# A fifth raw-weight place, down rows queued behind the last product, and three wide tiles in the first feed-forward

## The chip, the cores and the metric

The kernel runs on one core of one Trainium2 chip. The core has a matrix engine (TensorE, PE in the profile, its weight loads PEld), a vector engine (VectorE, DVE), a scalar engine (ScalarE, ACT), GpSimd (POOL) and SyncE (SP); each takes its instructions from a queue in order. SP issues nearly all of the loads. The metric is the device time of one execution in microseconds, as the median of several runs.

## What is computed

A decoder layer on 512 tokens of width 1024, in float32: a feed-forward, a mixer (dilated attention and a gated linear recurrence side by side), and a second feed-forward, each between two RMS norms and added to the residual with the factors of the reference.

```python
def swiglu(x, w_gate, w_up, w_down):
    return (jax.nn.silu(x @ w_gate) * (x @ w_up)) @ w_down

f = swiglu(rms_norm(h, ffn1_norm_pre[l]), ffn1_w_gate[l], ffn1_w_up[l], ffn1_w_down[l])
h = h + 0.5 * rms_norm(f, ffn1_norm_post[l])
u = rms_norm(h, mix_norm_pre[l])
proj = u @ w_in[l]
...
h = h + rms_norm(merged @ w_out[l], mix_norm_post[l])
f = swiglu(rms_norm(h, ffn2_norm_pre[l]), ffn2_w_gate[l], ffn2_w_up[l], ffn2_w_down[l])
h = h + 0.5 * rms_norm(f, ffn2_norm_post[l])
```

D_FF is 2816, so the gate and up matrices have 22 tiles of 128 columns each.

## The kernel before

**Numbers.** Every operand of a large product is split into a high part and a low part (`split`, lines 302 to 304: a copy on ACT at 303, a subtraction on DVE at 304), and a product is high x high + high x low + low x high, three matmuls of the same place.

**Seven products.** A gate tile and an up tile, over two halves of the 1024 inputs and two halves of the 512 tokens, form a 2 x 2 block product that is done with seven products p1 to p7 in place of eight. The operands of the seven are sums and differences of the quarters: of the activations once (`x_forms`, `forms_of`), of the weights for each tile (`w_forms`, line 685: four adds on DVE and four splits). A tile's weight forms take three places of `w8` (of four) and one of `w4`.

A tile's seven products come in two forms with the same result. The narrow one (`seven_on`, line 734) has for each product and each of four k three matmuls of 256 columns (lines 730 to 732), 84 in all, and works in four half-banks of PSUM; ACT copies a half-bank at line 744 four times, DVE adds at 970 and 975. The wide one (`seven_wide`, line 765) has for each k one matmul of 512 columns, the high weights on the high and the low activations side by side (782), and one of 256 (783), 56 in all, and works in five whole banks. There a product's value is the sum of a bank's halves: ACT moves a bank to another at 788 (`move`, three times a tile), copies a half at 794 and DVE adds the other half at 796 (`fold`, four times), and `sum_of` makes two adds at 804 and 806 (twice). Both run p1, p5, p6, p2, p7, p3, p4; the third product writes on the bank of a copy that was taken behind the first, the fifth and the seventh likewise behind the third and the fifth.

**Feed-forward.** `ffn_order` (67) writes out the order: the first 6 tiles of the first feed-forward (3 of the second) as plain products, then for every tile f the weight forms of tile f + 1 (`prep`), the tile's seven products (`prod`, 961), and behind them a step of the down projection. The 22 rows of down are in parts 0 to 3 (16 rows, also done as seven products, `down7`, 1055: rows of three matmuls of 512 columns at 1065 to 1067) and a last part of 6 rows, which `last_product` does behind all tiles. The steps of a part are done behind the tiles in `STEPS_AT`; in the first feed-forward part 1 stands behind tiles 9 to 12, part 2 behind 13 to 16, part 3 behind 17 to 20. A step needs the weight forms of `d_forms` (991) and its start values, which ACT puts into the `aux` banks at 1053; its results go to the `ea` tile or to `facc` at 1070.

**What sets the order.** The framework's scheduler queues the instructions of each engine ahead of time, by a precedence that follows the program's text and by when its own model takes them to be ready. `tc.high_priority(offset=n)` moves a block forward by n; weight forms have 100 (`AHEAD`), copies out of PSUM 200 (`EVAC`). `tc.issue_after(x)` puts the block's instructions on the engine of x behind x in its queue, without a wait. In the second feed-forward three such edges exist: the rows of `down7` stand behind `state["product"]`, the last product so far (1064); the weight forms of the next tile stand behind the last split of `d_forms` (1110 to 1111, 1104 to 1107); and the late activation forms behind the last copy (`rest`, 939 to 944). None of the three is in the first.

**Loads.** The weights come as one stream of blocks of 128 x 1024 in the order of use (`stream_plan`, `raw_of`, 235). Each goes on SP to one of four places `raw`; the load waits until DVE and ACT have read what stood there. The first 8 blocks, of 512 columns, are loaded by `fetch_start` (278) into the four places, but for the very first, which has a tile `first_t` together with the small constants `sm`. The first norm's sum of squares `acc` and its root `r1` have a pool of their own, `npool`. `r1` is read last by the plain tile 5 (956 and 958).

Of the kernel before, what the change touches and what calls it, by code (L numbers as in the profile page):

```python
# [10 lines left out]
F32 = mybir.dt.float32  # L11
# [5 lines left out]
P = 128  # L17
T = 512
# [2 lines left out]
NF = 22  # L21
FF_PARTS = ((0, 4), (4, 8), (8, 12), (12, 16), (16, 22))
NSTD = {1: 6, 2: 3}
WIDE = {1: (), 2: (9, 13, 17)}

SEVEN = range(4)
STEPS_AT = {1: ((6, 7, 7, 8), range(9, 13), range(13, 17), range(17, 21)),
# [3 lines left out]
EPS = 1e-6  # L31
HB = 256
RAW_W = 1024
NEG = -1.0e30

FIRST_ON = {1: 5, 2: 5}
# [67 lines left out]
def stream_plan():  # L104

    plan = []

    def down(n, a, half):
        for kk in range(part_blocks(a)):
            plan.append((("down", n, a, half, kk), 1024))  # L110

    def ffn(n):
        for ev in ffn_order(n):
            if ev[0] == "std":
                plan.append((("gate", n, ev[1]), 1024))
                plan.append((("up", n, ev[1]), 1024))
            elif ev[0] == "prep":
                plan.append((("gu", n, ev[1]), 2048))
            elif ev[0] == "prepd":
                for q in SEVEN_RAW[ev[2]]:  # L120
                    plan.append((("dq", n, ev[1], q), 1024))
        for half in range(2):
            down(n, len(FF_PARTS) - 1, half)

    def qk(h):
        for g in range(NG):
            plan.append((("pair", g * 4 + h, 12 + g * 4 + h), 2048))

    ffn(1)
    del plan[:4]  # L130
    for k in range(KC):
        plan.insert(k, (("start", k), 512))
    for k in range(4):
        plan.append((("v", 0, k), 1024))
    for q in ("g0", "g1", "u0", "u1"):
        plan.append((("vq", q), 2048))
    for h in range(NH):
        qk(h)
    for c in range(0, KC, 2):
        plan.append((("pair", 52 + c, 53 + c), 2048))  # L140
    for m in range(0, KC, 2):
        plan.append((("attn", m), 1024))
    for what, h in LRU_ORDER:
        if what == "gates":
            plan.append((("lru", h), 1024))
        elif (what, h) in PAIRED:
            plan.append((pair_key(what, h), 2048))
        else:
            for c in GATE1[h] if what == "gate1" else (2 * h, 2 * h + 1):
                plan.append((("in", COLUMN[what] + c), 1024))  # L150
    for m in range(KC):
        plan.append((("rec", m), 1024))
    for half in range(2):
        for kk in range(4):
            plan.append((("out", half, kk), 1024))
    ffn(2)

    return [(key + (i,), RAW_W) if width > RAW_W else (key, width)
            for key, width in plan for i in (("lo", "hi") if width > RAW_W else ("",))]


def stream_groups():

    groups, cur, w = [], [], 0
    for key, width in stream_plan():
        if w + width > RAW_W or (cur and cur[0][0][0] == "start"):
            groups.append(cur)
# [12 lines left out]
SMALL_W = _o  # L180
# [4 lines left out]
def hybrid_layer(ctx: ExitStack, tc: tile.TileContext, xT: bass.AP, xN: bass.AP, wst: bass.AP,  # L185
# [4 lines left out]
    cpool = ctx.enter_context(tc.tile_pool(name="cpool", bufs=1))  # L190
    bpool = ctx.enter_context(tc.tile_pool(name="bpool", bufs=6))
    wpool = ctx.enter_context(tc.tile_pool(name="wpool", bufs=4))
    tpool = ctx.enter_context(tc.tile_pool(name="tpool", bufs=4))
    npool = ctx.enter_context(tc.tile_pool(name="npool", bufs=1))
    psum = ctx.enter_context(tc.tile_pool(name="psum", bufs=1, space=bass.MemoryType.PSUM))
    dpool = ctx.enter_context(tc.tile_pool(name="dpool", bufs=1, space=bass.MemoryType.DRAM))

    first_t = cpool.tile([P, 512 + SMALL_W], F32, name="first")
    sm = first_t[:, 512:]
    cst = cpool.tile([P, CONST_W], F32, name="cst")  # L200
    ones = cpool.tile([P, P], F32, name="ones")
    eps = cpool.tile([P, 1], F32, name="eps")
# [6 lines left out]
    def hm(m, sl=slice(0, T)):  # L209

        return hs["t"][m // 4][:, m % 4, sl]
# [21 lines left out]
    state = {"g": 0, "i": 0, "off": 0, "raw": None, "ahead": AHEAD, "split": None}  # L233

    def raw_of(key, dst=None):

        g, i = state["g"], state["i"]
        grp = groups[g]
        if i == 0:
            w = grp[-1][1] + grp[-1][2]  # L240
            raw = dst if dst is not None else wpool.tile([P, RAW_W], F32, name="raw", tag="raw", bufs=4)
            src = bass.AP(tensor=wst.tensor, offset=wst.offset + state["off"], ap=[[w, P], [1, w]])
            nc.sync.dma_start(raw[:, :w], src)
            state["raw"] = raw
            state["off"] += w * P
        k, o, w = grp[i]
        assert k == key, (k, key)
        src = state["raw"][:, o:o + w]
        if i + 1 == len(grp):
            state["g"], state["i"] = g + 1, 0  # L250
        else:
            state["i"] = i + 1
        return src

    def raw_two(key, dst=None):

        return [raw_of(key + (n,), None if dst is None else dst[:, i * RAW_W:(i + 1) * RAW_W])
                for i, n in enumerate(("lo", "hi"))]
# [10 lines left out]
    def w8():  # L269
        return wpool.tile([P, 2, 1024], F32R, name="w8", tag="w8", bufs=4)  # L270
# [6 lines left out]

    def fetch_start():

        raws = [wpool.tile([P, RAW_W], F32, name="raw", tag="raw", bufs=4) for _ in range(4)]  # L280
        wts = []
        for k in range(KC):
            raw = raws[k // 2][:, (k % 2) * 512:(k % 2) * 512 + 512]
            if k == 0:
                raw = first_t[:, :512]
                nc.sync.dma_start(hm(k), xT[k])
                nc.sync.dma_start(raw, first[:, :512])
            else:
                nc.sync.dma_start(raw, bass.AP(tensor=wst.tensor, offset=wst.offset + (k - 1) * 512 * P,
                                               ap=[[512, P], [1, 512]]))  # L290
                nc.sync.dma_start(hm(k), xT[k])
            if k % 2 == 0:
                wt = w8()
            o = (k % 2) * 512
            wts.append((wt[:, 0, o:o + 512], wt[:, 1, o:o + 512], raw))
        state["g"], state["off"] = KC, (KC - 1) * 512 * P
        return wts
# [14 lines left out]
    def tmp(name):  # L312
        return tpool.tile([P, T], F32, name=name, tag="t")
# [255 lines left out]
    def act_of(his, los):  # L569
        return Act([his[k // 4][:, k % 4, :] for k in range(8)], [los[k // 4][:, k % 4, :] for k in range(8)])  # L570
# [293 lines left out]
    def ffn(n, x, r, forms_x, apool, pss):  # L864
# [96 lines left out]
        def prod(f, w):  # L961
            g, u = tmp("g"), tmp("u")
            if f in WIDE[n]:
                seven_wide(t, w, *([x[:, h] for h in HALVES] for x in (g, u)), then=forms_left)
# [69 lines left out]
        def sum_at(p):  # L1034
            if p in outs:
                o, half, sign = outs[p]
                return quarter(o, half), sign
            return acts["ea"][:, extra.index(p)], 1.0

        def follows(a, p):  # L1040

            return a > 0

        def groups(i):
            return [(p, k) for p in SEVEN_STEPS[i] for k in range(2)]
# [9 lines left out]
        def down7(a, i, w):  # L1055
            x = sevens[a]
            gs = groups(i)
            for m, (p, k) in enumerate(gs):
                ps = seeded.pop((p, k))
                first = not follows(a, p)  # L1060
                for j in range(2):
                    xh, xl = (x[p][:, s_, j * HB + k * P:j * HB + k * P + P] for s_ in range(2))
                    wh, wl = (w[p][:, s_, j * T:(j + 1) * T] for s_ in range(2))
                    with tc.issue_after(state["product"]) if n == 2 else nullcontext():
                        PE.matmul(ps, xh, wh, start=first and j == 0, stop=False, skip_group_check=True)  # L1065
                        PE.matmul(ps, xh, wl, start=False, stop=False, skip_group_check=True)  # L1066
                        PE.matmul(ps, xl, wh, start=False, stop=j == 1, skip_group_check=True)  # L1067
                dst, sign = sum_at(p)
                with tc.high_priority(offset=EVAC):
                    ACT.activation(dst[:, k], ps, AF.Copy, scale=sign)  # L1070
                    if m + 3 < len(gs):
                        seed(a, *gs[m + 3])
            if a == SEVEN[-1]:
                merge(i)
# [64 lines left out]
    ap1 = ff1.enter_context(tc.tile_pool(name="act1", bufs=1))  # L1139
    new_h()  # L1140
    u1 = act_of(*act_two(ap1))
    acc = npool.tile([P, T], F32, name="acc", tag="acc", bufs=1)
    nc.scalar.dma_start(sm, first[:, 512:])
    warm(eps)

# [2 lines left out]
        PE.matmul(wu[:, :P], ones, ones, start=True, stop=True)  # L1148
    wts = fetch_start()
    pss = [acc_ps() for _ in range(4)]  # L1150
    r1 = npool.tile([P, T], F32, name="r", tag="r", bufs=1)
    for k in range(KC):
        wh, wl, raw = wts[k]
        if k == 0:
# [598 lines left out]
    grow5, _ = gains(ap2, 4)  # L1753
# [26 lines left out]
def _bias(table):  # L1780
# [10 lines left out]
    for hd in range(NH):  # L1791
        for g, (sl, s, d, m) in enumerate(((slice(0, 256), s0, 1, m0), (slice(256, 384), s1, 4, m1),
                                           (slice(384, 512), s1, 4, m2))):
            vals = table[:, g * 4 + hd][_bucket(np.maximum(s, 0) * d)]
            res[hd, :, sl] = np.where(m, vals, np.float32(NEG))
    return res
# [95 lines left out]
```

## Time and profile before

| | us |
|---|---|
| median of 3 runs | 1206.48 (1205.55 to 1207.29) |
| the profiled execution | 1206.06 |
| its span, first to last instruction | 1204.3 |
| PE busy in the span | 1196.5 |
| DVE busy | 1039.5 |
| ACT busy | 838.7 |
| POOL busy | 26.1 |

The span is what the rows of the trace cover; 1.76 us of the execution lie around it. A row of a group reads: line, engine, operation, out<-in by the program's names, shapes, count, then the busy time and the mean duration in ns, and the idle time of the engine ahead of it with what ended it. A row of the timeline has start and duration first. A row of a stretch has its bounds, its length and the busy time of PE, PEld, DVE, ACT and POOL (instructions in brackets), then the granted clock, the DMA share and GB/s. Matmuls are pipelined: the time that one costs is the distance between two starts, not its duration.

### The profile page before, as it was taken

To read this page: it belongs to the slowest core of one execution; us is meant where nothing else is said; L and a number is where in the kernel's file an instruction comes from. 1 tells how busy PE (TensorE), PEld (TensorE's weight loads), DVE (VectorE), ACT (ScalarE), POOL (GpSimd) and SP (SyncE) were. 2 spreads that over 40 slices of the span, in tenths; PEclk is the share of its full clock that TensorE was granted. 3 is DMA by queue.
4 is the path that set the end of the run, shared out by engine and by line. 5 is a ranking of instruction groups with operands and counts; after the bars stand their busy time and mean duration, and the time that the engine had idled before them with its cause. 6 is when DMAs were issued, how large, how long until landed. Compare 5 with 4: busy or idle time off the path is not lost.

```text
span 1204.3 us, 18736 instructions
## 1 busy us (share of the span) xinstructions
PE 1196.5 (99%) x7138; PEld 1065.4 (88%) x7138; DVE 1039.5 (86%) x1641; ACT 838.7 (70%) x1455; POOL 26.1 (2%) x51
## 2 busy tenths in 40 slices
PE   9999999999999999999999999999999999999997
PEld 8899999999888889888888888888899989898996
DVE  7999888889689899999978899874798888889974
ACT  7566787887566676777836988734566687878763
POOL 0000000000011000000000000000100000000000
PEclk9999999999999999999999999999999999999999
DMA  7234343434725232322323432235443333333441
GB/s 268 88 95 132 126 140 108 139 111 153 248 102 165 71 97 88 97 82 86 107 73 119 170 115 100 80 113 189 144 141 106 123 123 123 123 125 122 140 176 70
DMA packets 45819, 149.77 MB, mean 124 GB/s; under 512 B 5152, under 2 KB 8608, under 8 KB 45728
## 3 DMA queue, kind: packets, MB, share of 16 engines
q1 hardware_dynamic: 38160, 131.09, 33.5%
q0 software_dynamic: 7280, 17.30, 4.3%
q8 instruction: 56, 0.92, 0.3%
q14 instruction: 35, 0.29, 0.1%
q10 hardware_dynamic: 288, 0.17, 0.0%
HBM read 138.06 MB, written 6.29 MB: 120 GB/s over the span
## 4 chain that ended last, share of the span: by engine, by line
PE 98%; DVE 1%; ACT 0%; issue 0%; DVEq 0%; ACTq 0%
PE acc L782 12%; PE acc L730 9%; PE acc L732 9%; PE acc L731 9%; PE acc L316 7%; PE acc L318 7%; PE acc L317 7%; PE acc L783 6%; PE aux L1066 4%; PE aux L1065 4%; PE aux L1067 4%; PE acc L432 2%; PE acc L433 2%; PE acc L434 2%; PE aux L433 1%; PE aux L432 1%
## 5 line engine op out<-in xcount | busy, mean ns | idle before, releaser
L304 DVE TENSOR_TENSOR w<-raw,w 128x1024 fp32r<-128x1024 f32 (+1 forms) x272 | 297.1, 1100 | 34.1 <-ACT w L303 32.6
L303 ACT ACTIVATE w<-raw 128x1024 fp32r<-128x1024 f32 (+1 forms) x272 | 259.0, 958 | 86.5 <-PE acc L318 46.4
L732 PE MATMUL acc<-big,w 128*128 128x256 f32 x788 | 223.3, 283 | 0.0
L731 PE MATMUL acc<-big,w 128*128 128x256 f32 x788 | 223.2, 283 | 0.0
L730 PE MATMUL acc<-big,w 128*128 128x256 f32 x788 | 223.2, 283 | 0.0
L782 PE MATMUL acc<-big,w 128*128 128x512 f32 x452 | 161.4, 397 | 0.1
L731 PEld LDWEIGHTS acc<-big,w 128*128 128x128 f32 x788 | 151.2, 192 | 1.3
L730 PEld LDWEIGHTS acc<-big,w 128*128 128x128 f32 x788 | 151.2, 192 | 1.2
L732 PEld LDWEIGHTS acc<-big,w 128*128 128x128 f32 x788 | 151.2, 192 | 0.0
L783 PE MATMUL acc<-big,w 128*128 128x256 f32 x452 | 127.4, 282 | 0.0
L782 PEld LDWEIGHTS acc<-big,w 128*128 128x128 f32 x452 | 85.0, 188 | 19.5 <-PE acc L783 0.4
L1065 PE MATMUL aux<-w,xf 128*128 128x512 f32 x224 | 87.6, 391 | 0.0
L1066 PE MATMUL aux<-w,xf 128*128 128x512 f32 x224 | 87.6, 391 | 0.0
L1067 PE MATMUL aux<-w,xf 128*128 128x512 f32 x224 | 87.2, 389 | 0.0
L783 PEld LDWEIGHTS acc<-big,w 128*128 128x128 f32 x452 | 85.4, 189 | 0.3
L304 DVE TENSOR_TENSOR w<-s,w 128x1024 fp32r<-128x1024 f32 x51 | 62.3, 1221 | 2.3 <-ACT w L303 2.0
L303 ACT ACTIVATE w<-s 128x1024 fp32r<-128x1024 f32 x51 | 53.8, 1056 | 8.1 <-PE acc L732 4.9
L316 PE MATMUL acc<-xf,w 128*128 128x512 f32 (+1 forms) x168 | 59.1, 353 | 0.0
L318 PE MATMUL acc<-xf,w 128*128 128x512 f32 (+1 forms) x168 | 58.5, 349 | 0.0
L317 PE MATMUL acc<-xf,w 128*128 128x512 f32 (+1 forms) x168 | 58.5, 349 | 0.0
L782 PE MATMUL acc<-rb,w 128*128 128x512 f32 x152 | 55.5, 397 | 0.0
L1067 PEld LDWEIGHTS aux<-w,xf 128*128 128x128 f32 x224 | 42.1, 188 | 8.9
(464 smaller groups left out, 2917.3 us busy)
## 6 DMA issues: line engine op xcount, KB each, us to landing
raw<-in_w SPq DMA_DIRECT2D x232, 512.0 KB, 3.5
big<-xf POOLq DMA_DIRECT2D x6, 512.0 KB, 3.3
gains<-in_rows POOLq DMA_DIRECT2D x5, 512.0 KB, 5.6
h<-in_x SPq DMA_DIRECT2D x8, 256.0 KB, 5.0
h<-in_xn POOLq DMA_DIRECT2D x4, 512.0 KB, 5.9
kept_m<-h POOLq DMA_DIRECT2D x4, 512.0 KB, 2.9
vals<-in_w SPq DMA_DIRECT2D x4, 512.0 KB, 6.2
h<-kept_m POOLq DMA_DIRECT2D x4, 512.0 KB, 5.9
```

Source lines behind the costliest of these rows:

```text
L303: state["split"] = ACT.activation(dh, src, AF.Copy).ins
L304: state["low"] = DVE.tensor_sub(dl, src, dh.bitcast(F32)).ins
L316: PE.matmul(ps, wh, xh, start=first, stop=False)
L317: PE.matmul(ps, wh, xl, start=False, stop=False)
L318: PE.matmul(ps, wl, xh, start=False, stop=last)
L730: PE.matmul(ps, wh, xh, start=start and k == 0, stop=False, skip_group_check=True)
L731: PE.matmul(ps, wh, xl, start=False, stop=False, skip_group_check=True)
L732: state["product"] = PE.matmul(ps, wl, xh, start=False, stop=k == 3, skip_group_check=True).ins
L782: PE.matmul(part, wh, at(BOTH, k), start=start and k == 0, stop=False, skip_group_check=True)
L783: last = PE.matmul(cross, wl, at(0, k), start=False, stop=k == 3, skip_group_check=True)
L1065: PE.matmul(ps, xh, wh, start=first and j == 0, stop=False, skip_group_check=True)
L1067: PE.matmul(ps, xl, wh, start=False, stop=j == 1, skip_group_check=True)
```

## The change

Five edits. `RAW_N` gives the raw weights five places in place of four. To make room, `first_t` loses the 512 columns of the first block, which goes to its half of the first shared place, and `npool` goes away: `acc` and `r1` share a tile of the tag `e` of the first feed-forward's pool, the bank that `ea` takes afterwards. The edge behind `state["product"]` holds in both feed-forwards. And tiles 10, 14 and 18 of the first feed-forward are done by `seven_wide`.

```diff
@@ -21,7 +21,7 @@
-WIDE = {1: (), 2: (9, 13, 17)}
+WIDE = {1: (10, 14, 18), 2: (9, 13, 17)}
@@ -31,6 +31,7 @@
 RAW_W = 1024
+RAW_N = 5
@@ -191,12 +192,10 @@
-    npool = ctx.enter_context(tc.tile_pool(name="npool", bufs=1))
...
-    first_t = cpool.tile([P, 512 + SMALL_W], F32, name="first")
-    sm = first_t[:, 512:]
+    sm = cpool.tile([P, SMALL_W], F32, name="first")
@@ -238,7 +237,7 @@
-            raw = dst if dst is not None else wpool.tile([P, RAW_W], F32, name="raw", tag="raw", bufs=4)
+            raw = dst if dst is not None else wpool.tile([P, RAW_W], F32, name="raw", tag="raw", bufs=RAW_N)
@@ -277,12 +276,11 @@
-        raws = [wpool.tile([P, RAW_W], F32, name="raw", tag="raw", bufs=4) for _ in range(4)]
+        raws = [wpool.tile([P, RAW_W], F32, name="raw", tag="raw", bufs=RAW_N) for _ in range(4)]
...
             if k == 0:
-                raw = first_t[:, :512]
                 nc.sync.dma_start(hm(k), xT[k])
                 nc.sync.dma_start(raw, first[:, :512])
@@ -1061,7 +1059,7 @@
-                    with tc.issue_after(state["product"]) if n == 2 else nullcontext():
+                    with tc.issue_after(state["product"]):
                         PE.matmul(ps, xh, wh, start=first and j == 0, stop=False, skip_group_check=True)
@@ -1139,7 +1137,8 @@
-    acc = npool.tile([P, T], F32, name="acc", tag="acc", bufs=1)
+    norm = ap1.tile([P, 2, T], F32, name="acc", tag="e", bufs=1)
+    acc, r1 = norm[:, 0], norm[:, 1]
@@ -1148,7 +1147,6 @@
-    r1 = npool.tile([P, T], F32, name="r", tag="r", bufs=1)
```

## The prediction, made before the result

> **What bounds the kernel now.** I read the page's engine totals first, then a table of busy time by stage, and last the rows in which one tile of each form runs.
>
> ```profile
> span 1204.3 us, 18736 instructions
> PE 1196.5 (99%) x7138; PEld 1065.4 (88%) x7138; DVE 1039.5 (86%) x1641; ACT 838.7 (70%) x1455; POOL 26.1 (2%) x51
> ```
>
> PE is busy for all but 7.8 us of the span. The stages show where those 7.8 us are (the columns are PE, weight loads, DVE, ACT, POOL, then clock, DMA share and GB/s):
>
> ```profile
> 1.05:72.00 70.95, 70.94 (x313) 59.52 (x314) 64.47 (x92) 42.39 (x65) 0.00 (x0) 1.00 0.52 173
> 72.00:338.00 266.00, 266.00 (x1807) 247.70 (x1806) 231.67 (x313) 198.07 (x338) 3.82 (x7) 1.00 0.43 139
> 338.00:400.00 62.00, 61.82 (x286) 50.54 (x285) 57.78 (x98) 41.47 (x77) 9.52 (x19) 1.00 0.37 115
> 400.00:600.00 200.00, 199.82 (x1218) 176.54 (x1218) 187.60 (x407) 144.85 (x312) 0.00 (x0) 1.00 0.29 92
> 600.00:860.00 260.00, 260.00 (x1227) 217.26 (x1226) 205.01 (x306) 168.12 (x244) 5.05 (x9) 1.00 0.35 118
> 860.00:897.00 37.00, 36.97 (x286) 35.57 (x284) 33.74 (x55) 24.07 (x41) 4.82 (x7) 1.00 0.63 185
> 897.00:1165.00 268.00, 268.00 (x1850) 250.39 (x1849) 240.55 (x329) 204.75 (x347) 2.66 (x5) 1.00 0.40 131
> ```
>
> In the first feed-forward (72 to 338 us) PE is never idle, at full clock; the same holds in the second (897 to 1165). From 1.05 to 897 us PE is idle for 0.01 + 0.18 + 0.18 + 0.03 = 0.4 us; the rest of the 7.8 lies ahead of the first product or from 1165 us on, in the last product and the stores, which the change doesn't touch. So a load that comes earlier has at most 0.4 us of visible idleness to remove, and whatever else the change gains must come from fewer or shorter matmuls. DVE is the next engine: 231.67 of 266 us in the first feed-forward, 87%.
>
> **The wide tiles: what PE saves.** A narrow tile is 84 matmuls of 256 columns (7 products x 4 x 3), a wide one 28 of 512 and 28 of 256. The first row of a tile and the first of the down rows behind it give its length: tile 10 of the first feed-forward, narrow, and tile 9 of the second, wide.
>
> ```profile
> 136.78 0.28 PE L730 MATMUL acc<-big,w 128*128 128x256 f32 x1
> ...
> 146.85 0.40 PE L1065 MATMUL aux<-w,xf 128*128 128x512 f32 x1
> ```
>
> ```profile
> 982.29 0.39 PE L782 MATMUL acc<-big,w 128*128 128x512 f32 x1
> ...
> 992.17 0.40 PE L1065 MATMUL aux<-w,xf 128*128 128x512 f32 x1
> ```
>
> Narrow 10.07 us, wide 9.88 us: 0.19 saved per tile, 0.57 us for three. The Trainium skill (TensorE: Matmul & The Clock Gate, "Wait — 56ns, not 53.3ns?") has a warm matmul start N columns at 2.4 GHz plus about 2.5 ns behind the one before. Both forms stream 21,504 columns, so an estimate by that page is 28 fewer starts x 2.5 ns = 0.07 us per tile and 0.21 us in all instead of 0.57. The trace differs (0.19 per tile), and the trace decides.
>
> **The wide tiles: what ACT and DVE pay.** The narrow form copies four half-banks on ACT (line 744) and adds two on DVE. The wide form moves three whole banks (788), copies four halves (794), adds to those four (796) and makes two sums of two adds each (804 and 806, of the same size as 796). The rows are of all tiles, the second of one half of the narrow copies:
>
> ```profile
> L788 ACT ACTIVATE acc<-acc 128x512 f32<-128x512 f32 x66 | 38.9, 589 | 9.5 <-PE acc L783 6.9 <-DVE s L693 1.1 <-DVE c L796 1.1
> ...
> L744 ACT ACTIVATE c<-acc 128x256 f32<-128x256 f32 x62 | 23.5, 382 | 30.7 <-PE acc L732 30.5
> ...
> L796 DVE TENSOR_TENSOR c<-acc,c 128x256 f32<-128x256 f32 x44 | 18.5, 421 | 5.3 <-ACT c L794 5.2
> ...
> L794 ACT ACTIVATE c<-acc 128x256 f32<-128x256 f32 x44 | 16.6, 377 | 6.9 <-PE acc L783 6.9
> ```
>
> ACT: 3 x 0.589 + 4 x 0.377 - 4 x 0.382 = 1.75 us more per tile. DVE: 8 adds for 2, 6 x 0.42 = 2.5 us more. The SiLU and the product behind it are done in one piece for two, which takes a little off both; I leave that out. The stretches from the first matmul of tiles 10, 14 and 18 to that of the tile after, and of tile 9 in the second feed-forward, already wide, show what room there is:
>
> ```profile
> 136.78:152.32 15.54, 15.54 (x109) 14.59 (x108) 12.86 (x17) 12.05 (x23) 0.00 (x0) 1.00 0.38 122
> 196.22:211.76 15.54, 15.54 (x109) 14.58 (x108) 12.50 (x17) 12.05 (x23) 0.00 (x0) 1.00 0.41 123
> 255.66:271.20 15.54, 15.54 (x109) 14.59 (x108) 12.47 (x18) 12.02 (x23) 0.00 (x0) 1.00 0.40 119
> 982.29:997.63 15.34, 15.34 (x81) 13.08 (x80) 13.40 (x22) 12.50 (x23) 0.00 (x0) 1.00 0.30 104
> ```
>
> DVE comes to 12.86 + 2.5 = 15.4 us in a stretch that will last 15.35, and to 15.0 in the two others; ACT to 13.8. So DVE is full in tile 10, and what it can't do there falls into tile 11. What is late next is the weight forms of tile 11, whose second product needs the form that DVE line 304 makes from the sums:
>
> ```profile
> 148.25 1.23 DVE L304 TENSOR_TENSOR w<-s,w 128x1024 fp32r<-128x1024 f32 x1 [0.17 <-ACT w L303]
> ```
>
> ```profile
> 153.75 0.28 PE L730 MATMUL acc<-big,w 128*128 128x256 f32 x1
> ```
>
> It is ready at 149.48 and used at 153.75: 4.27 us of cover against 2.5 us of added work. If that cover were gone, each microsecond of lateness would be one of PE. I cost the DVE side at nothing.
>
> The ACT side is tighter. Each of the three moves has to end within one product, 9.88 / 7 = 1.41 us after the product before it, since the next product but one writes on the bank that was moved into (in the narrow form, out of). Two places of the second feed-forward show it kept and missed: the move of wide tile 9, and a narrow copy two tiles later that stands behind a weight split on ACT.
>
> ```profile
> 984.15 0.61 ACT L788 ACTIVATE acc<-acc 128x512 f32<-128x512 f32 x1
> ```
>
> ```profile
> 1012.00 1.05 ACT L303 ACTIVATE w<-raw 128x1024 fp32r<-128x1024 f32 x1
> 1012.95 0.38 ACT L744 ACTIVATE acc<-acc 128x256 f32<-128x256 f32 x1
> ```
>
> ```profile
> 1013.21 0.28 PE L732 MATMUL acc<-big,w 128*128 128x256 f32 x1
> 1013.38 0.39 PE L730 MATMUL acc<-tx,w 128*128 128x256 f32 x1
> 1013.60 0.28 PE L731 MATMUL acc<-tx,w 128*128 128x256 f32 x1
> ```
>
> The first product of tile 9 ends at 982.29 + 1.41 = 983.70, the third may begin at 985.11, and the move is over at 984.76: 0.35 us to spare. Behind the wide tile the copy ends at 1013.33 and PE's next two starts take 0.39 us for the usual 0.24 (two pitches of 10.07 / 84): 0.15 us lost. The chain of waits has a like row 59.39 us later, in the tile that lies two behind wide tile 13, and I price it the same:
>
> ```profile
> 1072.87 0.28 PE acc L730
> ```
>
> Two such losses for three wide tiles there, so I take 2 x 0.15 = 0.30 us here. Bounds: none (0), and the mishap of the first rival.
>
> **Down rows behind the last product.** In the first feed-forward only one down matmul runs ahead of its place, alone among the products of tile 6:
>
> ```profile
> 73.33 0.40 PE L1065 MATMUL aux<-w,xf 128*128 128x512 f32 x1
> ```
>
> Moved back, it costs its own length in either place, so 0. The edge orders only PE's queue; no DMA, SP, POOL, ACT or DVE instruction is in it. Queued behind a held row are only the other down rows and the next tile, and PE stands in that order already. The cost would differ from nothing only where products wait and the rows could have filled the hole; with 266.00 of 266 us busy there is no such hole. Bounds 0, and at worst the 0.30 us above a second time.
>
> **The fifth place and the moved tiles.** SP's loads wait nearly always for DVE to free a raw place, and the two rows after that are the release and the next use of the bank that now holds the norm and then the sums of the down rows:
>
> ```profile
> SPq L243 <- DVE w L304: 760.7, 168, 20.1
> ```
>
> ```profile
> L958 DVE TENSOR_TENSOR u<-acc,r x6: 683/688/692, 31.9 to 72.1; 128x512 f32<-128x512 f32 x6
> ```
>
> ```profile
> L1070 ACT ACTIVATE ea<-aux x64: 575/596/603, 83.7 to 1129.4; 128x512 f32<-128x512 f32 x64
> ```
>
> The last read of the norm ends at 72.8 us and the first write of the sums is at 83.7, so sharing the bank adds a wait that 10.9 us of products cover. The first raw tile moves from a place of its own into half of a shared one, with the same two DMAs in the same order on SP, so 0. One more load in flight lets SP run ahead by one load; the total of bytes is the same. Gain: between 0 and the 0.4 us of idleness, plus what idle time doesn't show: 20 paired tiles between the feed-forwards (12 of queries and keys, 4 of gates, 4 of branches), at 0.15 us each if all lost that and all got it back, 3.0 us. Loss: with weights landing sooner, splits can be queued on ACT ahead of copies where they weren't, at 0.15 us for each of 16 + 19 + 20 paired tiles, 8.3 us. Both ends are far off. The nearest rows are the two feed-forwards, where neither happens beyond two tiles, so I take 0.
>
> **Sum.** -0.57 + 0.30 + 0 + 0 = -0.27 us. The profiled execution took 1206.06 us (span 1204.3, 1.76 around it), 0.42 below the median of the three runs. It comes to 1205.8 for such an execution and 1206.2 for a median.
>
> **Rivals.** *ACT late at the moves (slower).* The edges that keep weight and activation splits apart in the second feed-forward stay out of the first. There, ACT does stand idle in its queue for DVE in front of other work:
>
> ```profile
> 130.78 0.63 ACT L303 ACTIVATE w<-raw 128x512 fp32r<-128x512 f32 x1 [1.78 <-DVE raw L697]
> ```
>
> Were such a split to stand ahead of a move, the move would end 1.78 + 0.63 + 0.59 = 3.00 us after its product for the 1.41 it has: 1.59 us of PE. Once in each wide tile that is 4.8 - 0.57 = +4.2 us, 1210.7. It decides from the point where ACT comes free later than 1.41 - 0.59 = 0.82 us after the product. For it: DVE full in tile 10, and ACT's splits wait for DVE. Against it: the copies have precedence over splits in the order, and the already wide tiles and 16 narrow ones lose nothing.
>
> *The fifth place frees the middle (faster).* If the whole bound of 3.0 us and the 0.4 came back: 1206.48 - 0.57 - 3.4 = 1202.5. For it: 760.7 us of waits on SP. Against it: those are waits of a queue that runs ahead, and PE waits for none.
>
> *The place does nothing and the three tiles pay for themselves in stalls:* 1206.5, inside no change.
>
> **How the numbers follow.** About 0.2% (2.4 us) is what a measurement of this kernel can tell from no change: below 1204.1 is faster, above 1208.9 slower. My forecast and the third rival end within it: 0.58 and 0.16, together 0.74. ACT late at the moves gets 0.16, the losses of the fifth place past 2.4 us 0.04, together 0.20 for slower; the fifth place freeing the middle, 0.06. The range leaves out the ends of both: from 1204.2 (2.3 us below the median: the 0.57 and half of the 3.4) to 1210.0, just short of the first rival's full price.
>
> **What would show it.** Three groups of matmuls at lines 782 and 783 in the first feed-forward, each with 9.9 us from first to last; PE busy for all of the stretch from 72 to about 337 us; DVE near 15 of 15.4 us in tile 10; no down row among products; the middle from 338 to 897 us as long as before. The prediction is wrong if a product in a wide tile starts over 0.3 us late behind a line 788 move that stands behind a split, if the weight forms of tile 11 are late, or if the middle changes by more than 2 us.

## The result and the profile after

The changed kernel takes 1209.24 us (median of 12 runs, 1208.67 to 1210.54) against 1206.49 (12 runs, 1205.55 to 1207.29): ratio 1.0024, 95% interval 1.0017 to 1.0032, 2.75 us slower. The time lies inside the range of the prediction and past the 1208.9 from which it called a result slower. The two profiled executions took 1206.06 and 1209.81 us, 3.75 apart; stage by stage the account below is of these two.

The engine totals of the changed kernel's page, and the shares of its chain that ended last:

```profile
span 1208.0 us, 18598 instructions
...
PE 1197.9 (99%) x7054; PEld 1060.5 (88%) x7054; DVE 1044.6 (86%) x1656; ACT 841.4 (70%) x1461; POOL 26.1 (2%) x51
...
PE 90%; DVE 6%; ACT 2%; issue 1%; DMA 1%; DVEq 0%; ACTq 0%
```

PE has 84 matmuls fewer (three wide tiles, 28 each) and is yet 99% busy for a longer span. It is idle for 10.1 us where it was for 7.8, which is 2.3 of the 3.75 us. The rest does not show in the totals: a matmul that had to wait also has a longer busy row (0.50 us for the usual 0.39 or 0.40 in rows below). The chain of work that ended last shows the change best: DVE has 6% of it, ACT 2% and loads 1%. Before, PE had 98% and DVE 1%.

Three stages of the changed kernel, each from one matmul to another, and the same three of before. The first feed-forward is taken from its first product in seven to its last product, the mixer from its first product to the one with `w_out`, the second feed-forward as the first. Columns are as in the prediction's table:

```profile
71.86:311.19 239.33, 238.42 (x1597) 219.81 (x1596) 216.31 (x292) 186.25 (x316) 3.29 (x6) 1.00 0.41 131
345.90:818.38 472.48, 471.02 (x2495) 402.56 (x2494) 418.39 (x739) 328.69 (x577) 11.14 (x22) 1.00 0.33 104
900.35:1168.87 268.52, 268.40 (x1850) 250.43 (x1849) 239.72 (x328) 204.97 (x347) 2.66 (x5) 1.00 0.39 128
```

```profile
71.89:309.63 237.74, 237.74 (x1681) 224.31 (x1680) 210.38 (x277) 182.44 (x309) 3.29 (x6) 1.00 0.41 133
343.97:815.26 471.29, 471.09 (x2496) 402.76 (x2495) 418.57 (x739) 328.88 (x577) 11.13 (x22) 1.00 0.33 104
897.23:1165.15 267.92, 267.92 (x1850) 250.35 (x1849) 240.47 (x329) 204.63 (x346) 2.66 (x5) 1.00 0.40 131
```

The first feed-forward is 1.6 us longer, though its matmuls need 0.57 less; the mixer is 1.2 longer and the second feed-forward 0.6, with the same instructions as before. The last product of the first feed-forward, between the first two rows, went from 34.34 to 34.70. Together that is 3.75 us, all of it; what lies ahead of these stages, between the mixer and the second feed-forward and behind them is as long as before, within 0.03 us each. The granted clock is 1.00 throughout. So the loss is spread over the kernel, and only the first feed-forward holds the new wide tiles. In the mixer DVE and ACT are as long busy as before (418.4 and 328.7 us for 418.6 and 328.9) and the loads bring as much: no work became slower there, it came later.

What PE waits for in the changed kernel (engine and line that wait, releaser; total us, times, longest). Before, the list had only the first row (ahead of the first product) and the sixth, with the same times:

```profile
PE aux L1147 <- DVE eps L228: 1.1, 1, 1.1
PE aux L1063 <- ACT aux L1051: 0.7, 1, 0.7
PE aux L1451 <- DVE xch L1448: 0.6, 1, 0.6
PE acc L780 <- ACT acc L786: 0.5, 1, 0.5
PE aux L314 <- ACT rec L301: 0.3, 1, 0.3
PE aux L548 <- DVE u L540: 0.2, 1, 0.2
PE acc L728 <- ACT acc L742: 0.2, 1, 0.2
```

Lines here are those of the changed kernel, one or two below those of before. Lines 1063 and 728 are the first feed-forward, lines 1451, 780 and 314 the mixer (1.4 us in three waits, each new). None stands in a wide tile of the first feed-forward.

**The wait of 0.7 us, followed back.** The chain of the changed kernel around it (start, us, what), with some pieces left out:

```profile
226.25 1.24 DVE w L302
227.49 0.02 issue
227.50 5.03 DMA raw<-in_w
...
232.56 0.04 DVE s L690
...
235.77 0.41 DVE g L968
236.18 0.61 DVE raw L695
...
236.81 1.58 ACT w L301 x2
...
238.91 0.60 ACT aux L1051
```

and the same moments on ACT and on PE:

```profile
236.22 0.42 ACT L969 ACTIVATE g<-g 128x256 f32<-128x256 f32 x1 [3.61 <-DVE g L968]
...
238.91 0.60 ACT L1051 ACTIVATE aux<-facc 128x512 f32<-128x512 f32 x1
```

```profile
238.51 0.39 PE L1065 MATMUL aux<-w,xf 128*128 128x512 f32 x1
239.56 0.50 PE L1063 MATMUL aux<-w,xf 128*128 128x512 f32 x1 [0.66 <-ACT aux L1051]
```

A raw load begins at 227.50, when a split on DVE (226.25 to 227.49) has freed its place, and lands at 232.53. The weight add of line 690 stands at the head of DVE's queue and waits for it; behind it, in order, stands DVE's part of the gate (`g`, 968). ACT therefore idles 3.61 us for `g`, then does the splits queued behind it, and the start values of the down row (1051) come last. PE should have gone on 0.23 us after 238.51 and goes on at 239.56. A load that is late for DVE reaches PE 7 us later, through two queues, at a down row that uses neither this load nor a weight form made from it.

### The profile page after: what moved, and what is told of

Read it like the earlier page. It is cut to its first block, busy times and chain, and to the rows that moved or that the text cites. A ratio compares the mean times of both kernels' runs of the same rounds, so it can differ in the third digit from the quotient of the medians.

```text
span 1208.0 us, 18598 instructions
## 1 busy us (share of the span) xinstructions
PE 1197.9 (99%) x7054; PEld 1060.5 (88%) x7054; DVE 1044.6 (86%) x1656; ACT 841.4 (70%) x1461; POOL 26.1 (2%) x51
## 4 chain that ended last, share of the span: by engine, by line
PE 90%; DVE 6%; ACT 2%; issue 1%; DMA 1%; DVEq 0%; ACTq 0%
PE acc L780 12%; PE acc L728 7%; PE acc L730 7%; PE acc L729 7%; PE acc L314 7%; PE acc L316 7%; PE acc L315 7%; PE acc L781 6%; PE aux L1063 3%; PE aux L1064 3%; PE aux L1065 3%; DVE w L302 2%; PE acc L432 2%; PE acc L430 2%; PE acc L431 2%; PE aux L430 1%
## 5 line engine op out<-in xcount | busy, mean ns | idle before, releaser
L728 PE MATMUL acc<-big,w 128*128 128x256 f32 x716 | 203.1, 284 | 0.1
L730 PE MATMUL acc<-big,w 128*128 128x256 f32 x716 | 202.6, 283 | 0.0
L729 PE MATMUL acc<-big,w 128*128 128x256 f32 x716 | 202.6, 283 | 0.0
L780 PE MATMUL acc<-big,w 128*128 128x512 f32 x524 | 187.1, 397 | 0.0
L781 PE MATMUL acc<-big,w 128*128 128x256 f32 x524 | 147.4, 281 | 0.0
L728 PEld LDWEIGHTS acc<-big,w 128*128 128x128 f32 x716 | 137.3, 192 | 1.9 <-ACT acc L742 0.4
L729 PEld LDWEIGHTS acc<-big,w 128*128 128x128 f32 x716 | 137.3, 192 | 1.1
L730 PEld LDWEIGHTS acc<-big,w 128*128 128x128 f32 x716 | 137.3, 192 | 0.0
L780 PEld LDWEIGHTS acc<-big,w 128*128 128x128 f32 x524 | 98.4, 188 | 22.6
L781 PEld LDWEIGHTS acc<-big,w 128*128 128x128 f32 x524 | 98.9, 189 | 0.4
L786 ACT ACTIVATE acc<-acc 128x512 f32<-128x512 f32 x75 | 44.3, 590 | 12.9 <-PE acc L781 10.4
```

The lines of the kernel that those rows point to most:

```text
L728: PE.matmul(ps, wh, xh, start=start and k == 0, stop=False, skip_group_check=True)
L729: PE.matmul(ps, wh, xl, start=False, stop=False, skip_group_check=True)
L730: state["product"] = PE.matmul(ps, wl, xh, start=False, stop=k == 3, skip_group_check=True).ins
L780: PE.matmul(part, wh, at(BOTH, k), start=start and k == 0, stop=False, skip_group_check=True)
L781: last = PE.matmul(cross, wl, at(0, k), start=False, stop=k == 3, skip_group_check=True)
```

## The experiments

All kernels are made from the kernel before. Ratios are to the kernel before, measured beside each, with 95% intervals. The theories told apart, with the letters that the expectations use: the fifth place by itself costs, by the order of the queues (A; for the mixer D); the wide tiles overload DVE (B); what the first feed-forward loses is only the order in which DVE and ACT take their work (C). Stage lengths in us, each from the start of one matmul to that of another in one profiled execution; the two middle columns are the last product of the first feed-forward and the mixer. The profiled execution lies between 1.51 us below (hw_both) and 0.91 above (places) its kernel's median, so a difference of a few tenths in a single row says little. What repeats says more: the first feed-forward takes 237.73 or 237.74 us in the four kernels that have four places and no wide tile there; the mixer takes 470.50 to 471.29 us with four places and 472.23 to 472.76 with five.

| kernel | places, wide tiles | median | first FF | last product | mixer | second FF |
|---|---|---|---|---|---|---|
| before | 4, none | 1206.49 | 237.74 | 34.34 | 471.29 | 267.92 |
| after | 5, three | 1209.24 | 239.33 | 34.70 | 472.48 | 268.52 |
| moves | 4, none | 1206.20 | 237.74 | 34.34 | 471.00 | 267.93 |
| places | 5, none | 1209.56 | 239.78 | 34.33 | 472.62 | 268.53 |
| hold | 4, none | 1206.37 | 237.73 | 34.33 | 471.10 | 268.11 |
| hold_wide | 4, three | 1208.54 | 239.84 | 34.34 | 470.97 | 268.43 |
| places_hold | 5, none | 1208.74 | 239.18 | 34.34 | 472.23 | 268.53 |
| all_behind | 5, three | 1208.64 | 237.53 | 35.18 | 472.70 | 268.63 |
| all_both | 5, three | 1208.54 | 237.81 | 34.75 | 472.76 | 268.63 |
| places_hold_behind | 5, none | 1208.62 | 238.09 | 34.33 | 472.67 | 268.53 |
| hw_both | 4, three | 1207.55 | 238.30 | 34.33 | 470.52 | 268.39 |
| five_mixer | 5 in the mixer, none | 1207.43 | 237.73 | 34.34 | 472.51 | 267.93 |
| five_first | 5 in the first FF, three | 1205.82 | 237.72 | 34.33 | 470.50 | 268.26 |

### One part of the change at a time

**moves**: the tile moves alone, the raw weights left with four places.

```diff
-    first_t = cpool.tile([P, 512 + SMALL_W], F32, name="first")
-    sm = first_t[:, 512:]
+    sm = cpool.tile([P, SMALL_W], F32, name="first")
...
-                raw = first_t[:, :512]
...
-    acc = npool.tile([P, T], F32, name="acc", tag="acc", bufs=1)
+    acc, r1 = (lambda t: (t[:, 0], t[:, 1]))(ap1.tile([P, 2, T], F32, name="acc", tag="e", bufs=1))
...
-    r1 = npool.tile([P, T], F32, name="r", tag="r", bufs=1)
```

> The tiles are moved (first raw block into the shared place, norm and root into the bank of the down sums) and the raw weights keep four places. Only 12 places of DVE's queue and one of ACT's stand differently than before. Theory A (the fifth place itself, which sets 175 places of DVE's queue and 103 of ACT's differently, makes the loss) and theory B (the wide tiles overload DVE in the first feed-forward) both expect 0, within 0.5 us of before. Over 1 us slower would put the loss on the moved tiles.

1206.20 against 1206.35, ratio 0.9998 (0.9989 to 1.0007). The moved tiles cost nothing. They do not change the order either: by the rows of the trace DVE, ACT and PE take the same instructions in the same order as before, and the 12 places of DVE's queue and the one of ACT's that the expectation counts differ only in the names of the tiles that were moved.

**places**: the same, and the fifth place.

```diff
-            raw = dst if dst is not None else wpool.tile([P, RAW_W], F32, name="raw", tag="raw", bufs=4)
+            raw = dst if dst is not None else wpool.tile([P, RAW_W], F32, name="raw", tag="raw", bufs=5)
```

> The moved tiles and the fifth place, no wide tile in the first feed-forward, no hold. Theory A: +2.5 to +3.5 us on before (the 2.75 of the whole change and the 0.2 to 0.6 that the wide tiles give), with new PE stalls in the first feed-forward, the mixer and the second feed-forward. Theory B: +1.2 to +2.2 us, what the trace of after loses behind the first feed-forward, and no new stall between 72 and 338 us.

1209.56, ratio 1.0024 (1.0014 to 1.0034). Against moves it is 3.36 us slower, and the two kernels hold the same instructions; what differs is the number of places, and with it the order that the scheduler wrote into the queues. Against before, places has DVE's queue changed in 175 places (those 12 of other names among them), ACT's in 103 and PE's in 27. The PE timeline of places shows one of the 27:

```profile
107.45 0.28 PE L732 MATMUL acc<-big,w 128*128 128x256 f32 x1
107.93 0.72 PE L1065 MATMUL aux<-w,xf 128*128 128x512 f32 x2 [0.21 <-ACT w L303]
108.50 0.28 PE L730 MATMUL acc<-big,w 128*128 128x256 f32 x1
```

Two matmuls of a down row were queued among the products of a tile, ahead of their weights: 0.48 us from one start to the next for the usual 0.12. This happens three times in the stage. In the mixer, the first pair of a head shows the other kind of loss. ACT in moves, then in the changed kernel:

```profile
441.00 0.58 ACT L788 ACTIVATE acc<-acc 128x512 f32<-128x512 f32 x1
441.60 1.28 ACT L1426 ACT_TABLE_LOAD   x1
442.90 0.40 ACT L1426 ACTIVATE facc<-facc,stn 128x128 f32<-128x128 f32 x1
```

```profile
442.72 1.28 ACT L1424 ACT_TABLE_LOAD   x1
444.02 0.40 ACT L1424 ACTIVATE facc<-facc,stn 128x128 f32<-128x128 f32 x1
...
444.42 0.58 ACT L786 ACTIVATE acc<-acc 128x512 f32<-128x512 f32 x1
```

and PE in the changed kernel:

```profile
444.25 0.28 PE L781 MATMUL acc<-big,w 128*128 128x256 f32 x1
445.05 0.50 PE L780 MATMUL acc<-rb,w 128*128 128x512 f32 x1 [0.52 <-ACT acc L786]
```

With four places the move of a wide product stands ahead of the table load for the exponentials; with five it stands behind the load and the first exponential. The move ends at 445.00, and PE, which would have begun at 444.37, begins at 445.05 (0.52 us of this as idle time): the loss in the first rival's manner, at a move, but in a stage where no tile was made wide. The mixer's two other waits are of the same kind. A matmul that waits for `xch` stands in PE's queue at 446.98, among the products of a tile and ahead of its DVE work, and in moves only from 451.8 on; and at 655.62 a weight split of 1.06 us stands on ACT ahead of the split of `rec`, in moves behind it. That these orders cause the waits is read from the rows; no kernel moved one of these instructions alone.

**hold** and **hold_wide**: down's rows behind the last product in both feed-forwards, with four places; then with tiles 10, 14 and 18 wide too.

```diff
-                    with tc.issue_after(state["product"]) if n == 2 else nullcontext():
+                    with tc.issue_after(state["product"]):
```

```diff
-WIDE = {1: (), 2: (9, 13, 17)}
+WIDE = {1: (10, 14, 18), 2: (9, 13, 17)}
```

> The hold alone, four places. One down matmul of tile 6 moves behind the tile's products, nothing else in any queue. Both theories: 0, within 0.3 us of before.

> The hold and the wide tiles 10, 14 and 18 with four places. Theory A: -0.2 to -0.6 us (3 x 0.19 us less a few stalls of 0.1 to 0.15), PE stalls between 72 and 338 us below 0.4 us. Theory B: +1 to +2 us, with the stalls of after near the down rows behind tile 16 and tile 18 (0.9, 0.4 and 0.4 us).

hold: 1206.37, ratio 0.9999 (0.9990 to 1.0008), no cost. hold_wide: 1208.54, ratio 1.0016 (1.0007 to 1.0024). So the wide tiles lose by themselves too, without a fifth place: 237.73 to 239.84 in the stage, +2.11, where their matmuls save 0.57; some 2.7 us of stalls. The largest is two tiles behind wide tile 10. The chain of hold_wide there, and the copy as PE sees it:

```profile
166.47 3.61 DMA raw<-in_w
...
170.10 0.69 DVE s L693
170.79 0.61 DVE tt L935
171.41 0.02 issue
171.43 0.03 ACT xf L303
171.46 0.94 issue
172.40 0.37 ACT c L744
```

```profile
172.81 0.38 PE L730 MATMUL acc<-big,w 128*128 128x256 f32 x1 [0.89 <-ACT c L744]
```

The same form as before: a load lands, DVE's weight add had stood waiting for it at the head of the queue, the late activation form `tt` behind it comes late, ACT's split of that form (171.43 to 172.49) stands ahead of the copy of a product, and PE stands idle for 0.89 us (it starts 1.04 us late).

### The fifth place with the hold, and the edges of the second feed-forward

**places_hold**: moves, the fifth place and the hold, without wide tiles (the edits of places and hold). It asks how much of the changed kernel's loss comes from the wide tiles.

> The fifth place, the moved tiles and the hold, no wide tile in the first feed-forward. In the run with the fifth place alone, three down rows stand among products and each makes PE wait 0.37 us for its weight split. If that is so, the hold takes 3 x 0.37 = 1.1 us off the first feed-forward (239.78 to about 238.7 us) and leaves the mixer (+1.3) and the second feed-forward (+0.6) as they are: +2.1 us on before. If the place costs the stage otherwise, the first feed-forward stays near 239.8 and the total at +3.2.

1208.74 against 1206.73, ratio 1.0017 (1.0007 to 1.0026). The hold takes 0.6 off the stage (239.78 to 239.18), not the 1.1 expected: it ends the three waits among the products, but the stage has late starts in other places for them. The hold is worth something only with five places. The rest of the loss stays, and the changed kernel, with wide tiles, is hardly longer there (239.33). The two losses are no sum; that both come from one order of the queues would explain it, and is not shown by this run.

**all_behind** and **all_both**: the whole change, and in the first feed-forward the edge that puts the next tile's weight forms behind the splits of the down rows; then the edge on the late activation forms too.

```diff
                 forms[ev[1:]] = d_forms(*ev[1:])
-                if n == 2:
+                if True:
                     behind[:] = [state["split"], state["low"]]
```

```diff
-                    with tc.high_priority(offset=AHEAD), tc.issue_after(state["copied"]) if n == 2 else nullcontext():
+                    with tc.high_priority(offset=AHEAD), tc.issue_after(state["copied"]) if n == 2 or a else nullcontext():
...
-                if n in (2,):
+                if n == 2 or a:
```

> The whole change, and the edge of the second feed-forward that puts a tile's weight forms behind the last split of the down forms now in the first too. Theory C (what the first feed-forward loses is the order of DVE's and ACT's queues: adds that wait for a load, and splits, stand in front of copies): its stage falls from 239.34 to 237.2 to 238.0 us, the total by 1.3 to 2.1 us. Theory B (DVE has too much work there with the wide tiles): the stage stays within 0.5 us of 239.3. Mixer and second feed-forward as in the change by both.

> As the one before, and from part 1 on also the second edge of the other feed-forward: the late activation forms behind the last copy. Theory C: the stage at or below that of the one before, 237.2 to 237.7 us (237.74 less 0.57, and up to 0.5 of stalls). Theory B: near 239.3 us.

all_behind: 1208.64, ratio 1.0018 (1.0009 to 1.0027); all_both: 1208.54, ratio 1.0019 (1.0010 to 1.0029). The one edge takes the first feed-forward from 239.33 to 237.53, 0.21 below before, with three wide tiles and the work of DVE unchanged (216.06 us for 216.31). The stage of all_behind:

```profile
71.97:309.51 237.54, 237.54 (x1598) 219.91 (x1596) 216.06 (x293) 186.34 (x315) 3.30 (x6) 1.00 0.38 130
```

So DVE did not have too much to do; it did it in a poor order. The second edge adds nothing that can be told. The total hardly gains: the mixer and the second feed-forward stay long, and the last product of all_behind is 0.84 longer than before (35.18); 0.5 of it is a wait of PE for a DVE split of an activation form, and I have no kernel for it.

**places_hold_behind**: all_behind without its wide tiles, and **hw_both**: hold_wide with both edges.

> The fifth place, the moved tiles, the hold and the weight-form edge in the first feed-forward, no wide tile there. Theory C, with the wide tiles worth what the rows of one tile give: the stage is 237.53 + 0.57 = 238.1 us, within 0.2, the rest as in the other runs with five places (mixer +1.2 to 1.5, second feed-forward +0.6). Rival: the wide tiles give nothing once ordered (stage 237.5) or cost (below 237.5).

> Four places, hold and wide tiles, with both edges in the first feed-forward. Theory C: the stage falls from 239.84 to 237.2 to 237.9 us and, since mixer and second feed-forward with four places are within 0.5 us of before, the total comes to -0.5 to +0.3 us on before. Theory B: the stage stays near 239.8, the total near +2.2 us.

places_hold_behind: 1208.62 against 1206.36, ratio 1.0018 (1.0009 to 1.0028). Its stage is 238.09, all_behind's 237.53: with the edge three wide tiles take 0.56 off, the 0.57 of the prediction. Against places_hold (239.18) the edge alone takes 1.1 off the stage with five places and no wide tile, and PE has no idle time left in it. But the two kernels' totals do not differ (ratios 1.0017 and 1.0018), so that most of the place's loss in this stage is one of order rests on the two profiled executions. hw_both: 1207.55 (1206.04 to 1209.54) against 1206.73, ratio 1.0009 (0.9999 to 1.0019), not told apart from no change. Its mixer is back at 470.52 with four places. Its first feed-forward comes down from 239.84 to 238.30, but not to the 237.81 of all_both, which has the same edges and five places, nor to the 237.9 expected at most: edges that mend one order mend another less. Its one profile is of its fastest execution, so the 238.30 may be low.

### The fifth place in one stage only

The fifth place gets a tag of its own that every fifth load takes, and only while a stage is loading: the mixer's loads in **five_mixer** (with the hold, no wide tiles), the first feed-forward's in **five_first** (with the hold, three wide tiles and the weight-form edge).

```diff
+    def raw_place():
+        state["n"] += state["five"]
+        fifth = state["five"] and state["n"] % 5 == 1
+        return wpool.tile([P, RAW_W], F32, name="raw", tag="raw5" if fifth else "raw", bufs=1 if fifth else 4)
...
-            raw = dst if dst is not None else wpool.tile([P, RAW_W], F32, name="raw", tag="raw", bufs=4)
+            raw = dst if dst is not None else raw_place()
```

> The fifth place is used by the loads of the mixer alone (a place of its own that every fifth load there takes); both feed-forwards have four; hold, no wide tile in the first. Theory D (the fifth place orders the mixer's queues worse by itself): first feed-forward 237.7 us, mixer 472.2 to 472.8 us, with the PE waits of 0.7 and 0.8 us in the first head. Rival (the mixer's loss is what is left over from the feed-forward before it, whose last loads stand differently): mixer 470.9 to 471.3 us and the total as before.

> The fifth place is used by the loads of the first feed-forward alone; hold, wide tiles and the weight-form edge there. Theories C and D together: first feed-forward 237.5 us, mixer 470.5 to 471.2 us, second feed-forward 267.9 to 268.5 us, in sum -0.5 to +0.3 us on before. Rival (the mixer's loss follows from the feed-forward): mixer near 472.6 us, +1 us on before.

five_mixer: 1207.43 against 1206.36, ratio 1.0009 (1.0000 to 1.0019). The total can hardly be told from no change, but its stages can: its feed-forwards are as before, and its mixer is 472.51, 1.2 longer. Its list of PE's waits has the mixer's three of the changed kernel, to the tenth (lines six or seven further on):

```profile
PE aux L1458 <- DVE xch L1455: 0.6, 1, 0.6
PE acc L786 <- ACT acc L792: 0.5, 1, 0.5
PE aux L320 <- ACT rec L307: 0.3, 1, 0.3
```

five_first is the counterpart: 1205.82 (11 runs, 1205.06 to 1206.68) against 1206.36, ratio 0.9996 (0.9987 to 1.0005). Its stages:

```profile
71.64:309.36 237.72, 237.72 (x1598) 219.97 (x1596) 216.05 (x293) 186.33 (x315) 3.30 (x6) 1.00 0.38 128
343.69:814.19 470.50, 470.43 (x2496) 402.24 (x2494) 418.51 (x739) 329.01 (x577) 11.17 (x22) 1.00 0.31 105
896.15:1164.41 268.26, 268.24 (x1851) 250.37 (x1849) 240.60 (x329) 204.77 (x346) 2.67 (x5) 1.00 0.38 131
```

PE has no hole in the first feed-forward, and the mixer shows none of the three waits. So the 1.2 us of the mixer go with the mixer's use of the fifth place and come back without it. Against all_behind, which differs only in where the fifth place is used, it gains 2.8 us by the medians, and the intervals do not overlap. So what the place still costs once the edge is there, it costs behind the tiles of the first feed-forward. This is the best version found, 3.4 us below the changed kernel, but not shown to be faster than before: the interval holds 1. Its first feed-forward has three wide tiles and is as long as before's 237.74, so about half a microsecond of their gain is still lost there, in six starts late by 0.11 us and less.

## Why the prediction was wrong

**What bounds the kernel: right, and used wrongly.** PE still bounds it, and the fuller PE is, the less can be gained by an earlier load: at most the 0.4 us. But a PE with no hole is not protected against a loss. I read "266.00 of 266" as cover; it says only that in this one order of the queues every copy and split comes in time, by margins such as 0.35 us.

**What a wide tile saves: right.** Tile 10 of the changed kernel, from its first row to the first down row behind it:

```profile
136.94 0.39 PE L780 MATMUL acc<-big,w 128*128 128x512 f32 x1
...
146.82 0.40 PE L1063 MATMUL aux<-w,xf 128*128 128x512 f32 x1
```

9.88 us as forecast, and 0.56 us for three between places_hold_behind and all_behind. The Trainium skill (TensorE: Matmul & The Clock Gate, "Wait — 56ns, not 53.3ns?") would have given an estimate of 0.21 for three; the pair of runs bears out the trace's rows and not the page's 2.5 ns for each start.

**What ACT and DVE pay: a quarter too high in sum, wrong in place.** DVE does 5.9 us more in the stage and ACT 3.8 (forecast 7.5 and 5.25, with the smaller SiLU work left out). But DVE is busy for 13.29 us in tile 10 and not 15.4:

```profile
136.94:152.32 15.38, 15.38 (x81) 13.06 (x80) 13.29 (x22) 12.29 (x23) 0.00 (x0) 1.00 0.35 108
```

I had added the new work to what stood in that stretch before; in the new order other work stands elsewhere. Nor was DVE's total the limit, as all_behind shows.

**The moves of the wide tiles: right.** The first move of tile 10 ends at 139.42, and the third product may begin at 136.94 + 2 x 1.41 = 139.76: 0.34 us to spare, and PE waited for no move in this stage.

```profile
138.81 0.61 ACT L786 ACTIVATE acc<-acc 128x512 f32<-128x512 f32 x1
```

**The stalls behind the wide tiles: a term mis-sized.** "Two such losses for three wide tiles there, so I take 2 x 0.15 = 0.30 us here." The kind was right (narrow copies and start values behind splits, two tiles later), the size was not: 2.7 us in hold_wide, the one kernel that has the wide tiles and the hold alone. The two rows I priced from are of the second feed-forward, which has the edges that the first lacks; I named the missing edges only in the rival, and there put the loss at the moves. The edge of all_behind alone takes 1.8 us off. The rival "ACT late at the moves", at 1210.7, came nearest in time and held the mechanism, with the splits that wait for DVE; its place was wrong, and so was its cause, a DVE that is full.

**The hold: right.** Nothing with four places; with five it takes back 0.6 of what the fifth place costs, because only then are rows queued early.

**The fifth place: the step that failed.** "Both ends are far off. The nearest rows are the two feed-forwards, where neither happens beyond two tiles, so I take 0." It costs 3.36 us alone (places against moves) and accounts for the mixer's whole 1.2 us. I had the mechanism in hand as the loss bound (splits queued ahead of copies) and gave it 4 in 100, because the rows of before show no such loss. They can't: they are the rows of the order that four places gave. A place more changed the queues in 175, 103 and 27 places, the mixer's among them, where the change has no edit of its own. That the scheduler takes each load to be there at another time, and so orders everything behind it anew, is how I explain it; the runs show the new order and not the scheduler's reason. That the time lies inside the range all the same is luck: the upper end was set by the price of ACT late at the moves, and PE waited for no move in the first feed-forward. My sign for the place's loss (the middle as long as before) did catch it, but the bound I gave it, 2 us, was wider than the 1.2 that were lost.

**Still open.** The second feed-forward is 0.6 to 0.7 longer in every kernel that has five places there. The trace shows where: PE starts late at 1140.92 and at 1153.90 in the changed kernel, by 0.22 and 0.10 us at each, and by some 0.1 at a few starts more; at 1153.90 ACT's split of a late activation form, which had waited 1.50 us for DVE, stands ahead of the copy that PE needs, and in moves it does not. No kernel changed that order. With four places the stage is 0.3 to 0.5 longer in the kernels with three wide tiles in the first feed-forward (hold_wide, hw_both, and five_first, which has the fifth place in the first feed-forward only), for which I have no reason. The last product is longer only with five places and wide tiles together (after, all_behind, all_both). And whether a single edge in the mixer (the move ahead of the table load) would bring back part of its 1.2 us was not tried.

## What to carry to other kernels

In a kernel whose queues are written ahead of time by a scheduler, a buffer count is an edit of the instruction order: cost it as a reshuffle of every queue, with losses of the size of the margins that PE lives on, and try it one stage at a time. Price a stall from a stage that has the same ordering edges as the stage that is changed. When PE is 99% busy both before and after, compare the distances between the starts of its matmuls and the chain's shares; the busy totals show only a part.

## What the runs showed that I had not expected

Two kernels with the same instructions and the same bytes, with one place of 128 x 1024 more, differ by 3.36 us of 1206. And the place does what it is for, only not where it counts: DVE's waits for raw loads come down from 11 us in all to 8, and yet one of those left began PE's longest wait in the first feed-forward. In the changed kernel DVE waited 1.40 us for the load that landed at 232.53, because that load could begin only when DVE freed a place, as the chain shows; it took 5.03 us against 3.6 for the median of its kind:

```profile
232.56 0.69 DVE L690 TENSOR_TENSOR s<-raw 128x512 f32<-128x512 f32 x1 [1.40 <-DMA raw<-in_w]
```

```profile
raw<-in_w SPq DMA_DIRECT2D x232, 512.0 KB, 3.6
```
